# Output projection of a hybrid encoder block: row tiles normalised in the next step, gates three tiles ahead, operand sums stored by GpSimd

## The chip, the cores and the metric

The kernel runs on one core of a Trainium2 chip, in one launch. The metric is the device time of an execution in microseconds (us), median of several. The engines are named as the profile names them: PE (TensorE: matrix products and transposes), DVE (VectorE), ACT (ScalarE), POOL (GpSimd) and SP (SyncE, which here only issues loads). SBUF is the on-chip memory, PSUM the banks in which PE leaves its results.

## The reference

One layer of an encoder over 2048 rows of 1024 channels, all float32. Half of the mixing width (512 channels) comes from an mLSTM in two directions, half from a Hyena convolution. Each half is normalised in groups, both are concatenated and go through one output projection, whose result is normalised and added to x; then comes an MLP with 4096 inner channels. What matters here is the stretch between the two:

```python
def rms_norm(x, w):
    y = xf * rsqrt(mean(xf * xf, axis=-1) + EPS)
    return y * w
...
# ym: mLSTM output times its output gate, yz: convolution output times its gate
y  = concat(group_rms(ym, 4 heads), group_rms(yz, 8 groups))      # 2048 x 1024
x1 = x + rms_norm(y @ w_out, norm_mix_post)
h  = rms_norm(x1, norm_mlp_pre)
out = x1 + rms_norm(relu(h @ w_mlp_in)**2 @ w_mlp_out, norm_mlp_post)
```

## The kernel before

PE multiplies in three passes to keep float32 precision: each operand is split into a high and a low part (`hi`, `lo`), and `mm3` issues hi x hi, hi x lo and lo x hi (lines L159 to L161 of every group of rows). A split is a cast on ACT (L166) and a subtraction on DVE or POOL (L169).

`out_proj` works on 16 row tiles of 128 rows, in a loop of 18 steps (`for i in range(18)`). Five parts belong to a tile h:

- `gate(h)`: loads `rd` and `xg`, four matmuls into the bank `py` (L1247), DVE's product with `xg` gives `zt` (tile name `yz`), ACT's square (L1252), DVE's sum over groups (L1254), root and reciprocal (L239, L241), and POOL's scaling (L1257).
- `mixed(h)`: loads `ymt` and `ot`, POOL's product (L1329), then the same normalisation.
- `turned`: four transposes of such a tile into the bank `ptp` (L1263) and the split into `yt`, the operand of the projection.
- `part(po, e, y, k0)`: twelve matmuls of a half of the channels into accumulator bank `po[e]`. Three banks `po` and three banks `tp` (shared by `py`, `ptp` and `pto`) rotate.
- `finish(h, po)`: loads x into `xt`; ACT squares the accumulator (L1205), DVE scales it (L1211), POOL adds the residual (L1212): `xt` becomes x1 and is stored. `normed(h)`: ACT's square of x1 (L1351), DVE's scaling (L1354) into the tile `xo`. `turn_out(h)`: two tiles later in the loop, eight transposes into `pto`, and DVE's product (L1365) back into `xo`.

The MLP uses a fast form of a 2 x 2 block product with seven products, so `turn_out` of each odd tile also makes four sums and differences of blocks of an even and an odd tile (POOL, L1380 to L1383, in `tb` and `xo`) and stores five operands to `ht` in DRAM, each 256 KB as 512 rows of 512 bytes. The first step of the MLP (`first_step`, tiles `hm`, `cb`, `pm`, `m`) begins inside the loop's last two steps; its weights are prepared on POOL from tile 12 on (L1480 to L1490).

In the loop the order on PE, DVE and ACT is the order in which the code is written (`manual_schedule`). POOL's and SP's orders are set by a scheduler. Every engine takes its instructions in order. `self.load` issues from SP's queue, `self.store` from ACT's queue: there an issue is an instruction of ACT, and stands with its wait ahead of what follows on ACT. In the step of a tile, PE does: transposes of the next tile's `yz`, part 0 with `yz`, a gate's four matmuls, transposes of the next `ymt`, part 0 with `ym`, part 1 with `yz`, the eight transposes of `turn_out`, part 1 with `ym`.

Of the kernel before, what the change touches and what calls it, by code (L numbers as in the profile page):

```python
# [17 lines left out]
D = 1024  # L18
# [129 lines left out]
class Builder:  # L148
# [1127 lines left out]
    def out_proj(self, c):  # L1276
        tc, io = self.tc, self.io
        pe, dve, act, pool = self.pe, self.dve, self.act, self.pool
        wp = self.hq
        wl = c.enter_context(tc.tile_pool(name="owl", bufs=2))  # L1280
        gc = ExitStack()
        wk = gc.enter_context(tc.tile_pool(name="owk", bufs=2))
        ps = c.enter_context(tc.tile_pool(name="opt", bufs=3, space=PSUM, side="right"))
# [58 lines left out]
        def finish(h, po):  # L1342
            xt = wl.tile([128, D], F32, tag="xt", name="xt")
            self.load(xt, self.rows(io["x"][0], h))
            x1 = wl.tile([128, D], F32, tag="xo", name="xo", bufs=3)
            self.post(wl, po, wb, (x1[:, 0:512], x1[:, 512:1024]), xt, "po", dve if h == 15 else pool)
            self.store(self.x1[h], xt)
            return x1, xt

        def normed(h, x1, xt):  # L1350
            act.activation(x1, xt, AF.Square, accum_out=ss1[:, h:h + 1])  # L1351
            act.activation(ss1[:, h:h + 1], ss1[:, h:h + 1], AF.Sqrt, scale=1.0 / D, bias=self.eps)
            dve.reciprocal(r1[:, h:h + 1], ss1[:, h:h + 1])
            dve.tensor_scalar(x1, xt, r1[:, h:h + 1], None, ALU.mult)  # L1354
            return x1

        def turn_out(h, xn):

            xv = xn.rearrange("p (k c) -> p k c", k=8)
            for half in range(2):  # L1360
                ks = slice(4 * half, 4 * half + 4)
                pt = ps.tile([128, 512], F32, tag="tp", name="pto", bufs=3).rearrange("p (q c) -> p q c", q=4)
                for q in range(4):
                    pe.transpose(pt[:, q, :], xv[:, 4 * half + q, :], self.eye)
                dve.tensor_tensor(xv[:, ks, :], pt, self.nw1[:, ks].unsqueeze(2).to_broadcast([128, 4, 128]), ALU.mult)  # L1365
# [12 lines left out]
            b11, b21, b12, b22 = ev[:, 0:4, :], ev[:, 4:8, :], xv[:, 0:4, :], xv[:, 4:8, :]  # L1378
            ta, tb = (self.cb.tile([128, 2, 4, 128], F32, tag="cb", name="tb", bufs=9) for _ in range(2))
            pool.tensor_tensor(ta[:, 0], b12, b11, ALU.subtract)  # L1380
            pool.tensor_tensor(ta[:, 1], b22, ta[:, 0], ALU.subtract)
            pool.tensor_tensor(tb[:, 0], b21, ta[:, 1], ALU.subtract)
# [24 lines left out]
        self.load(wb, io["norm_mix_post"].partition_broadcast(128))  # L1407
        xns = {}
        staged = self.first_operands(scratch)
        for i in range(18):  # L1410
            with tc.manual_schedule(engines={mybir.EngineType.PE,mybir.EngineType.DVE,mybir.EngineType.Activation}):
                if i == 0:
                    ys[1] = mixed(1)
                    zs[2] = gate(2)
                    part(pos[0], 0, ym[0], 0)
                    ym[1] = turned(ys.pop(1), 1, 1)
                    ys[2] = mixed(2)
                elif i + 2 < 16:
# [3 lines left out]
                if i < 16:  # L1422
                    if i > 1:
                        pos[i] = banks()
                    if i > 1:
                        part(pos[i], 0, yz[i], 4)
# [480 lines left out]
```

## Time and profile before

| | |
|---|---|
| median of 3 runs | 2765.75 us (2764.37 to 2766.28) |
| profiled execution | 2761.93 us, span 2759.2 us, mean granted clock of PE 0.977 |
| PE busy | 2614.5 us, 95% of the span |
| DVE, ACT, POOL busy | 1523.9, 1220.6, 1189.9 us (55, 44, 43%) |
| 1225 to 1465 us (the loop): PE, POOL busy | 222.4 and 137.0 of 240 us |
| 1465 to 1525 us (first step of the MLP): PE busy | 46.1 of 60 us, at a clock of 0.83 |

The profile comes from one execution, a little under the median. In its rows a line such as `ptp<-eye,yz` reads "written from". A bracket `[4.52 <-POOL yz L1257]` behind a row is the time that the engine stood idle just before, and what ended it. Rows with a q (ACTq, SPq, POOLq) are instructions of that engine's queue, such as issues of DMAs. A profiled line of the changed kernel can stand one to two lines off its number before.

### The profile page before, as it was taken

Reading aid. Unit: us, or ns where it says so; the run is one execution under the profiler, and the core shown is the slowest. Engines: PE = TensorE matmul, PEld = TensorE weight load, DVE = VectorE, ACT = ScalarE, POOL = GpSimd, SP = SyncE. Lnnn points to the kernel's source line nnn. Section 1 sums busy time; section 2 is a strip of 40 time slices with the busy share of each in tenths; the row PEclk is TensorE's granted clock in tenths of the full one; section 3 lists DMA queues with packets and bytes.
Section 4 is the critical chain, followed back from the end, with each engine's and each line's share of the span. In section 5 each row is a group of like instructions: output and inputs, shape, how many; then the busy total and the mean of one; then the engine's idle time right before and its main releaser. Section 6 shows DMA issues by size and latency. Waiting matters only on the chain.

```text
span 2759.2 us, 35826 instructions
## 1 busy us (share of the span) xinstructions
PE 2614.5 (95%) x12422; PEld 2140.2 (78%) x12422; DVE 1523.9 (55%) x2598; ACT 1220.6 (44%) x2237; POOL 1189.9 (43%) x941
## 2 busy tenths in 40 slices
PE   6999999999899998789997999989999999999998
PEld 4778878777788888776775788868888888888876
DVE  5676643777546664664445445464445443543578
ACT  6355544555444444543334454454444233222244
POOL 1211114554225543424566777777773241311232
PEclk8999999999999999989998999999999999999999
DMA  6233336655566657956765544454446563445546
GB/s 169 62 91 108 115 115 211 196 186 178 195 218 179 183 164 243 269 177 195 229 189 190 180 141 163 151 207 167 144 151 229 198 184 108 121 143 158 188 154 227
DMA packets 307187, 474.22 MB, mean 172 GB/s; under 512 B 37814, under 2 KB 166198, under 8 KB 305984
## 3 DMA queue, kind: packets, MB, share of 16 engines
q1 hardware_dynamic: 231952, 333.24, 38.9%
q10 hardware_dynamic: 70304, 125.98, 12.1%
q0 software_dynamic: 4752, 12.72, 2.1%
q8 instruction: 99, 1.62, 0.2%
q14 instruction: 80, 0.66, 0.1%
HBM read 297.65 MB, written 174.20 MB: 171 GB/s over the span
## 4 chain that ended last, share of the span: by engine, by line
PE 44%; DMA 5%; DVE 4%; POOL 3%; issue 2%; ACT 1%; SPq 0%; ACTq 0%; DVEq 0%; POOLq 0%
PE pm L160 13%; PE pm L161 13%; PE pm L159 13%; DMA mb<-mrow 1%; DMA ymt<-ym 1%; POOL cb L169 1%; PE po L159 1%; PE po L160 1%; PE po L161 1%; PE py L1247 1%; DVE cb L169 1%; DMA m<-in_w_mlp_out_dram 1%; DVE hm L169 1%; DVE hm L1832 0%; PE pa L983 0%
## 5 line engine op out<-in xcount | busy, mean ns | idle before, releaser
L166 ACT CAST cb<-m 128x1024 fp32r<-128x1024 f32 (+1 forms) x346 | 281.3, 847 | 441.9 <-PE pm L159 388.1
L169 DVE TENSOR_TENSOR cb<-m,cb 128x1024 fp32r<-128x1024 f32 (+1 forms) x222 | 240.1, 1119 | 298.7 <-ACT cb L166 298.3
L159 PE MATMUL pm<-hm,cb 128*128 128x512 f32 x896 | 355.0, 396 | 16.9 <-ACT hm L166 5.8
L160 PE MATMUL pm<-hm,cb 128*128 128x512 f32 x896 | 355.1, 396 | 10.9 <-DVE hm L169 7.1
L161 PE MATMUL pm<-hm,cb 128*128 128x512 f32 x896 | 353.7, 395 | 0.0
L160 PE MATMUL pm<-cb 128*128 128x512 f32 x880 | 343.3, 390 | 7.2 <-DVE cb L169 7.2
L159 PE MATMUL pm<-cb 128*128 128x512 f32 x880 | 342.1, 389 | 1.0 <-DVE cb L169 1.0
L161 PE MATMUL pm<-cb 128*128 128x512 f32 x880 | 342.5, 389 | 0.0
L169 POOL TENSOR_TENSOR cb<-m,cb 128x1024 fp32r<-128x1024 f32 x124 | 273.7, 2221 | 73.3 <-ACT cb L166 62.5
L1644 DVE TENSOR_TENSOR m<-pm,m 128x512 f32<-128x512 f32 x224 | 154.3, 690 | 242.7 <-PE pm L161 218.5
L159 PE MATMUL pt<-hn,w 128*128 128x512 f32 x640 | 270.4, 423 | 1.0 <-ACT hn L487 0.9
L169 POOL TENSOR_TENSOR raw<-raw,hi 128x512 fp32r<-128x512 f32 x160 | 205.3, 1295 | 121.9 <-ACT hi L166 85.6
L160 PE MATMUL pt<-hn,w 128*128 128x512 f32 x640 | 254.7, 398 | 0.3 <-DVE hn L488 0.2
L161 PE MATMUL pt<-hn,w 128*128 128x512 f32 x640 | 253.2, 396 | 0.0
L159 PEld LDWEIGHTS pm<-hm,cb 128*128 128x128 f32 x896 | 171.1, 191 | 56.7 <-ACT hm L166 6.8
L160 PEld LDWEIGHTS pm<-hm,cb 128*128 128x128 f32 x896 | 170.9, 191 | 51.2 <-DVE hm L169 10.3
L160 PEld LDWEIGHTS pm<-cb 128*128 128x128 f32 x880 | 165.2, 188 | 44.7 <-DVE cb L169 10.6
L161 PEld LDWEIGHTS pm<-hm,cb 128*128 128x128 f32 x896 | 170.9, 191 | 36.4
L159 PEld LDWEIGHTS pm<-cb 128*128 128x128 f32 x880 | 165.1, 188 | 35.8 <-ACT junk L1817 1.4
L161 PEld LDWEIGHTS pm<-cb 128*128 128x128 f32 x880 | 165.2, 188 | 34.2
L1648 ACT ACTIVATE m<-m 128x512 f32<-128x512 f32 x128 | 80.5, 630 | 219.4 <-DVE m L1644 217.3
L597 DVE SCALAR_TENSOR_TENSOR yc<-pt,cw,yc 128x511 f32<-128x511 f32 (+1 forms) x280 | 135.1, 516 | 51.2 <-ACT yc L591 49.2
(321 smaller groups left out, 5604.2 us busy)
## 6 DMA issues: line engine op xcount, KB each, us to landing
ga<-m ACTq DMA_DIRECT2D x96, 512.0 KB, 4.4
m<-ga SPq DMA_DIRECT2D x96, 512.0 KB, 3.8
d<-st ACTq DMA_DIRECT2D x64, 512.0 KB, 4.0
m<-in_w_mlp_in_dram SPq DMA_DIRECT2D x62, 512.0 KB, 3.7
m<-in_w_mlp_out_dram SPq DMA_DIRECT2D x114, 256.0 KB, 4.0
raw<-d SPq DMA_DIRECT2D x96, 256.0 KB, 2.7
xt<-in_x_dram SPq DMA_DIRECT2D x32, 512.0 KB, 5.8
dk<-kst SPq DMA_DIRECT2D x32, 512.0 KB, 3.3
```

Of the source, the lines that this page charges most:

```text
L159: pe.matmul(ps, w[1], x[0], start=first, stop=False)
L160: pe.matmul(ps, w[0], x[1], start=False, stop=False)
L161: pe.matmul(ps, w[0], x[0], start=False, stop=last)
L166: self.act.copy(hi, src)
L169: (eng_lo or self.dve).tensor_tensor(lo, src, hi.bitcast(F32), ALU.subtract)
L597: dve.scalar_tensor_tensor(y[:, at], p[:, src], cw[:, ct, w:w + 1], y[:, at], ALU.mult, ALU.add)
L1247: self.pe.matmul(py, self.s1i[:, r], rd[:, r, :], start=r == 0, stop=r == 1)
L1644: dve.tensor_tensor(dst, a, b, ALU.add)
L1648: act.activation(g, g, AF.Relu)
```

## The change

- `normed(h)` moves out of the step of tile h, where it stood right behind `finish(h)`, into the next step, ahead of part 0 with `ym`. The store of x1 goes with it. `xo` has four places instead of three. The pool of `xt` and `xo` is opened just ahead of the loop, on the other side of SBUF.
- `gate` runs three tiles ahead instead of two (`yz` has three places; step 0 does two gates). `mixed(i + 2)` stands behind part 0 with `ym` instead of at the head of a step.
- Of the five operands of an odd tile, one (3) stays a store of ACT's queue; the four sums are issued by `pool.dma_start`, on POOL's own queue. The first goes out behind its sum, the other three behind the last sum.

PE has the same instructions in the same number.

```diff
@@ out_proj
-        wl = c.enter_context(tc.tile_pool(name="owl", bufs=2))
...
-            zt = wk.tile([128, 512], F32, tag="yz", name="yz")
+            zt = wk.tile([128, 512], F32, tag="yz", name="yz", bufs=3)
...
-            x1 = wl.tile([128, D], F32, tag="xo", name="xo", bufs=3)
+            x1 = wl.tile([128, D], F32, tag="xo", name="xo", bufs=4)
             self.post(wl, po, wb, (x1[:, 0:512], x1[:, 512:1024]), xt, "po", dve if h == 15 else pool)
+            return x1, xt
+
+        def normed(h, x1, xt):
             self.store(self.x1[h], xt)
-            return x1, xt
-
-        def normed(h, x1, xt):
             act.activation(x1, xt, AF.Square, accum_out=ss1[:, h:h + 1])
...
-            for i, src in ((3, b22), (5, ta[:, 0]), (7, b12), (6, ta[:, 1]), (4, tb[:, 0])):
-                out(i, src)
+            out(3, b22)
+            for i, src in ((5, ta[:, 0]), (6, ta[:, 1]), (4, tb[:, 0]), (7, b12)):
+                pool.dma_start(self.ht[h // 8, i - 1][:, :, 128 * t:128 * t + 128], src)
...
+        wl = c.enter_context(tc.tile_pool(name="owl", bufs=2, side="right"))
         for i in range(18):
...
                     ym[1] = turned(ys.pop(1), 1, 1)
+                    zs[3] = gate(3)
                     ys[2] = mixed(2)
-                elif i + 2 < 16:
-                    ys[i + 2] = mixed(i + 2)
                 if 0 < i < 15:
                     yz[i + 1] = turned(zs.pop(i + 1), i + 1, 0)
...
-                if 0 < i < 14:
-                    zs[i + 2] = gate(i + 2)
+                if 1 < i < 16:
+                    pos[i] = banks()
+                    part(pos[i], 0, yz[i], 4)
                 if 0 < i < 15:
+                    if i + 3 < 16:
+                        zs[i + 3] = gate(i + 3)
                     ym[i + 1] = turned(ys.pop(i + 1), i + 1, 1)
                 if 0 < i < 16:
+                    xns[i - 1] = normed(i - 1, *done)
                     part(pos[i], 0, ym[i], 0)
+                    if i + 2 < 16:
+                        ys[i + 2] = mixed(i + 2)
                     if i > 1:
                         part(pos[i], 1, yz[i], 4)
                 if 2 <= i:
                     turn_out(i - 2, xns.pop(i - 2))
                 if i < 15:
                     part(pos[i], 1, ym[i], 0)
-                    xns[i] = normed(i, *finish(i, pos.pop(i)))
+                    done = finish(i, pos.pop(i))
```

On ACT, in the step that turns tile 5 out, before: the five stores of operands (`xo_12969` is tile 5), then the accumulator of tile 7 (`xo_13244`), the store of its x1 and its square.

```order
L234 DMA ht_84<-xo_12969 512x1x128
L234 DMA ht_84<-tb_13219 512x1x128
L234 DMA ht_84<-xo_12969 512x1x128
L234 DMA ht_84<-tb_13219 512x1x128
L234 DMA ht_84<-tb_13220 512x1x128
L1205 ACTIVATE xo_13244,pss_13245<-po0_13145 128x512
L1205 ACTIVATE xo_13244,pss_13245<-po1_13146 128x512
L166 CAST yt_13279<-ptp_13280 128x512
L239 ACTIVATE po_sd_13250<-ps1_13248,eps_60 128x1
L234 DMA x1_83<-xt_13242 128x1024
L1351 ACTIVATE xo_13244,ss1_12126<-xt_13242 128x1024
```

The same place after (`xo_12986` is tile 5, `xo_13261` and `xt_13259` tile 7; `xg`, `gr64` belong to a gate):

```order
L234 DMA ht_84<-xo_12986 512x1x128
L1205 ACTIVATE xo_13261,pss_13262<-po0_13144 128x512
L1205 ACTIVATE xo_13261,pss_13262<-po1_13145 128x512
L166 CAST yt_13278<-ptp_13279 128x512
L239 ACTIVATE po_sd_13267<-ps1_13265,eps_60 128x1
L1252 ACTIVATE xg_13301<-yz_13304 128x512
L239 ACTIVATE gr64_sd_13312<-gss_13310,eps_60 128x8
L166 CAST yt_13278<-ptp_13317 128x512
L234 DMA x1_83<-xt_13259 128x1024
L1350 ACTIVATE xo_13261,ss1_12123<-xt_13259 128x1024
```

Four stores are gone ahead of L1205, and the store and the square of x1 stand behind the gate's square and the cast of the second `ptp`.

On POOL, around the sums of tile 5, before (`yz_13163` is tile 9, `ymt_13266` tile 10, `xt_13242` tile 7):

```order
L1257 TENSOR_TENSOR yz_13163<-yz_13163,gr64_r_13173 128x512
L1380 TENSOR_TENSOR tb_13219<-xo_12969,xo_12827 128x512
L1381 TENSOR_TENSOR tb_13219<-xo_12969,tb_13219 128x512
L1383 TENSOR_TENSOR xo_12969<-xo_12969 128x512
L1382 TENSOR_TENSOR tb_13220<-xo_12827,tb_13219 128x512
L1257 TENSOR_TENSOR ymt_13266<-ymt_13266,gr128_r_13276 128x512
L1212 TENSOR_TENSOR xt_13242<-xo_13244,xt_13242 128x512 x2
```

After (`ymt_13199` is tile 9, `ymt_13341` tile 10, `xt_13259` tile 7):

```order
L1257 TENSOR_TENSOR ymt_13199<-ymt_13199,gr128_r_13209 128x512
L1379 TENSOR_TENSOR tb_13236<-xo_12986,xo_12844 128x512
L1385 DMA ht_84<-tb_13236 512x1x128
L1380 TENSOR_TENSOR tb_13236<-xo_12986,tb_13236 128x512
L1382 TENSOR_TENSOR xo_12986<-xo_12986 128x512
L1381 TENSOR_TENSOR tb_13237<-xo_12844,tb_13236 128x512
L1385 DMA ht_84<-tb_13236 512x1x128
L1385 DMA ht_84<-tb_13237 512x1x128
L1385 DMA ht_84<-xo_12986 512x1x128
L1212 TENSOR_TENSOR xt_13259<-xo_13261,xt_13259 128x512
L1328 TENSOR_TENSOR ymt_13341<-ymt_13341,ot_13342 128x512
L1212 TENSOR_TENSOR xt_13259<-xo_13261,xt_13259 128x512
```

Four issues stand between the sums and the residual sum of the tile that was multiplied in that step, and the product of tile 10's `ymt` has come to stand behind them.

On SP, at the loop's beginning, before (`ot_12300` and `ymt_12299` are tile 2, the `xg` and `rd` are of gates):

```order
L231 DMA rd_12476<-d21_3602 128x2x512
L231 DMA xg_12264<-vp2_76 128x1x512
L231 DMA ot_12300<-vo_79 128x1x512
L231 DMA ymt_12299<-ym_82 128x1x512
L231 DMA rd_12609<-d21_3602 128x2x512
```

After (`ot_12317` and `ymt_12316` are tile 2, `xg_12264` and `xg_12300` of the gates of tiles 2 and 3):

```order
L231 DMA xg_12264<-vp2_76 128x1x512
L231 DMA xg_12300<-vp2_76 128x1x512
L231 DMA ymt_12316<-ym_82 128x1x512
L231 DMA rd_12475<-d21_3602 128x2x512
L231 DMA ot_12317<-vo_79 128x1x512
```

A second gate's `xg` now stands ahead of tile 2's `ot`, which rotates through the same two places.

More of the change, by code (lines that the diff above doesn't have):

```diff
@@ L1344, in finish @@
             self.load(xt, self.rows(io["x"][0], h))
-            x1 = wl.tile([128, D], F32, tag="xo", name="xo", bufs=3)
+            x1 = wl.tile([128, D], F32, tag="xo", name="xo", bufs=4)
             self.post(wl, po, wb, (x1[:, 0:512], x1[:, 512:1024]), xt, "po", dve if h == 15 else pool)
-            self.store(self.x1[h], xt)
             return x1, xt
         def normed(h, x1, xt):
+            self.store(self.x1[h], xt)
             act.activation(x1, xt, AF.Square, accum_out=ss1[:, h:h + 1])
@@ L1416, in out_proj @@
                     ym[1] = turned(ys.pop(1), 1, 1)
+                    zs[3] = gate(3)
                     ys[2] = mixed(2)
-                elif i + 2 < 16:
-                    ys[i + 2] = mixed(i + 2)
                 if 0 < i < 15:
                     yz[i + 1] = turned(zs.pop(i + 1), i + 1, 0)
[L1422 to L1426, printed above, removed]
-                if 0 < i < 14:
-                    zs[i + 2] = gate(i + 2)
+                if 1 < i < 16:
+                    pos[i] = banks()
+                    part(pos[i], 0, yz[i], 4)
                 if 0 < i < 15:
+                    if i + 3 < 16:
+                        zs[i + 3] = gate(i + 3)
                     ym[i + 1] = turned(ys.pop(i + 1), i + 1, 1)
                 if 0 < i < 16:
+                    xns[i - 1] = normed(i - 1, *done)
                     part(pos[i], 0, ym[i], 0)
+                    if i + 2 < 16:
+                        ys[i + 2] = mixed(i + 2)
                     if i > 1:
```

## The prediction

> **What bounds the kernel now.** I began with a table of the stage in stretches of 60 us, since the page's shares average over stages with different limits. The loop over row tiles runs from about 1225 us to 1470 us, the MLP's first step follows. Columns: PE, PEld, DVE, ACT and POOL busy (instructions), then the granted clock, the DMA share and GB/s.
>
> ```profile
> 1405.00:1465.00 60.00, 56.19 (x262) 43.84 (x261) 24.81 (x51) 22.22 (x53) 40.36 (x31) 1.00 0.53 165
> 1465.00:1525.00 60.00, 46.09 (x175) 35.24 (x174) 30.85 (x36) 22.58 (x34) 30.42 (x19) 0.83 0.66 223
> ```
>
> PE is the bound, and it is not full: it lacks 4 us of the loop's last 60 and 14 us of the 60 that follow. No other engine is near its limit; POOL is nearest, with 40 of 60 us just ahead of the MLP. What the change can win is therefore the sum of PE's gaps. The timeline of PE shows each with its releaser in brackets:
>
> ```profile
> 1251.95 1.11 PE L1263 MATMUL ptp<-eye,yz 128*128 128x128 f32 x4 [4.52 <-POOL yz L1257]
> 1291.73 0.50 PE L159 MATMUL po<-wo,yt 128*128 128x512 f32 x1 [0.71 <-DVE xo L1211]
> 1299.75 0.66 PE L1263 MATMUL ptp<-eye,yz 128*128 128x128 f32 x4 [1.32 <-DVE xo L1365]
> 1330.75 0.66 PE L1263 MATMUL ptp<-eye,yz 128*128 128x128 f32 x4 [1.27 <-DVE xo L1365]
> 1361.35 0.66 PE L1263 MATMUL ptp<-eye,yz 128*128 128x128 f32 x4 [1.14 <-DVE xo L1365]
> 1380.81 0.66 PE L1263 MATMUL ptp<-eye,yz 128*128 128x128 f32 x4 [4.62 <-POOL yz L1257]
> 1421.22 0.50 PE L159 MATMUL po<-wo,yt 128*128 128x512 f32 x1 [0.63 <-DVE xo L1211]
> 1429.25 0.66 PE L1263 MATMUL ptp<-eye,yz 128*128 128x128 f32 x4 [1.32 <-DVE xo L1365]
> 1451.90 0.50 PE L159 MATMUL po<-wo,yt 128*128 128x512 f32 x1 [1.36 <-DVE xo L1211]
> 1464.70 0.51 PE L159 MATMUL po<-wo,yt 128*128 128x512 f32 x1 [0.50 <-DVE xo L1211]
> ```
>
> They add up to 17.4 us. The two long ones cost more than their length, since the clock drops behind them (same columns as the first table):
>
> ```profile
> 1251.95:1256.00 4.05, 4.05 (x14) 3.39 (x15) 2.22 (x5) 0.88 (x2) 3.56 (x3) 0.61 0.53 184
> 1380.80:1385.00 4.20, 4.19 (x14) 3.38 (x15) 0.00 (x0) 0.00 (x0) 4.12 (x4) 0.59 0.57 196
> ```
>
> At 0.61 and 0.59 of full speed that is 4.05 x 0.39 + 4.20 x 0.41 = 3.3 us. So the loop loses 20.7 us in all. Why the short gaps arise stands in the waits (engine, line, what was awaited: total, times, longest) and on ACT's timeline:
>
> ```profile
> ACT xo L1351 <- POOL xt L1212: 56.3, 14, 5.8
> ...
> 1385.15 1.37 ACTq L234 DMA_DIRECT2D ht<-tb  x2
> 1386.63 0.60 ACT L1205 ACTIVATE xo<-po 128x512 f32<-128x512 f32 x1 [7.62 <-POOL tb L1382]
> ...
> 1467.74 1.06 ACT L1351 ACTIVATE xo<-xt 128x1024 f32<-128x1024 f32 x1 [4.07 <-POOL xt L1212]
> ```
>
> ACT takes its work in order. On every odd tile the stores of sums stand in its queue ahead of the next squares (L1205), and each must wait until POOL has made its sum; here ACT did no arithmetic for 7.62 us. Every tile has a second stop: the square of L1351 stands right behind its own tile's residual sum on POOL, 56.3 us of waiting in 14 tiles (not all of it harmful: the next squares may not be due yet). Both delay L1205, then DVE's L1211, which frees the accumulator's bank, and DVE's L1365, which frees a bank of the ring of three for transposes.
>
> **The change, part by part.** *The stores of sums leave ACT's queue* (4 of 5 on each of 8 odd tiles). This takes the first stop away: the remaining store needs only DVE's L1365. *Normalising one step later* takes the second away: the residual sum has most of a step to be made before ACT arrives at the square. With both gone I count the six gaps of the loop behind L1365 or L1211 up to 1430 us as gone: 0.71 + 1.32 + 1.27 + 1.14 + 0.63 + 1.32, or 6.4 us. Four places for normalised rows only pay for a tile's longer life, in space. The store of x1 and the last reader of xt move a step back too, so the load of x two tiles on goes out later: it still has over a step (14.6 us, below), and the waits show nothing of it.
>
> *Gate three tiles ahead.* Both long gaps are waits for yz, the gate's rows, on POOL. The second begins with a late load:
>
> ```profile
> 1375.17 1.28 POOL L1329 TENSOR_TENSOR ymt<-ymt,ot 128x512 f32<-128x512 f32 x1 [6.54 <-DMA ymt<-ym]
> ```
>
> POOL stood 6.54 us at the load of another tile, with yz queued behind it. One tile more of lead is 14.6 us (below), more than that, so yz is no longer what ends last: 4.52 + 4.62 + 3.3 us of clock = 12.4 us go. But the normed operand ymt is now the next one late. At the start its buffer comes from the ring xg that the gates use too, and the change gives it a later place there:
>
> ```profile
> 1234.71 0.69 DVE L1254 TENSOR_REDUCE gss<-xg 128x8 f32<-128x512 f32 x1 [0.75 <-ACT xg L1252]
> ...
> 1234.95 1.29 POOL L1329 TENSOR_TENSOR ymt<-ymt,ot 128x512 f32<-128x512 f32 x1 [3.03 <-DMA ymt<-ym]
> ...
> 1239.10 1.04 POOL L1257 TENSOR_TENSOR ymt<-ymt,gr_r 128x512 f32<-128x512 f32 x1 [1.85 <-DVE gr_r L241]
> ...
> 1239.54 1.88 PE L1247 MATMUL py<-rd,s1i 128*128 128x512 f32 x4
> 1241.26 0.60 PE L1263 MATMUL ptp<-eye,ymt 128*128 128x128 f32 x4
> ...
> ot<-vo SPq DMA_DIRECT2D x14, 256.0 KB, 4.8
> ```
>
> The last line is of the DMA view: the median load of ot lands 4.8 us after its issue. The buffer is free when the reduction of xg is done, at 1235.4, so the load lands at 1240.2. From the product to the end of the scaling an earlier ymt took 1234.95 to 1240.14, 5.2 us, with another scaling of POOL in between; I take 4.4 and get 1244.6. PE was at the transpose of ymt at 1241.26 and has one gate more to do before it (1239.54 to 1241.26, 1.7 us), so it arrives at about 1242.9: a new gap of 1.8 us. Its bounds are 0 and the 4.52 that it replaces. For the clock behind it I add 0.7, half of what followed the long gaps. The page "TensorE: Matmul & The Clock Gate" of the Trainium skill, Part 1, says that the clock falls only after an idle window of about 3.4 us; by that the 0.7 would be nothing and the time 0.7 us lower, which the two rows above, both behind longer gaps, can't decide.
>
> At the 4.62 gap the load of ymt remains late, now without yz behind it, and POOL has the MLP's two splits to do (2.45 us in a row below): between 0 and 4.6 us, and I take 1, since ymt is wanted later in a step than yz. In other steps, mixed stands later in its step: its loads come behind the gate's on SP's queue, its product behind the residual sum on POOL. Landing and chain (4.8 + 5.2 us) fit into the step of 14.6 us that it still has: nothing.
>
> *DMAs issued by POOL.* Before has none in this stage; POOL's own work there is (mean ns behind the bar):
>
> ```profile
> L1212 POOL TENSOR_TENSOR xt<-xo,xt 128x512 f32<-128x512 f32 x29 | 36.9, 1290 | 33.6 <-DVE xo L1211 33.6
> L1329 POOL TENSOR_TENSOR ymt<-ymt,ot 128x512 f32<-128x512 f32 x16 | 20.5, 1284 | 22.7 <-DMA ymt<-ym 20.4 <-issue 2.2
> L1257 POOL TENSOR_TENSOR ymt<-ymt,gr_r 128x512 f32<-128x512 f32 x16 | 16.6, 1040 | 13.8 <-DVE gr_r L241 13.7
> L1257 POOL TENSOR_TENSOR yz<-yz,gr_r 128x512 f32<-128x512 f32 x14 | 16.1, 1146 | 27.2 <-DVE gr_r L241 23.3 <-DMA ymt<-ym 3.9
> L1380 POOL TENSOR_TENSOR tb<-xo 128x512 f32<-128x512 f32 x6 | 7.7, 1288 | 4.5 <-DVE xo L1365 4.5
> ...
> L631 POOL DMA_DIRECT2D vp<-vst x96 | 61.2, 642 | 220.5 <-ACT vst L627 219.4 <-issue 1.1
> ...
> L185 POOL DMA_DIRECT2D cs1k<-in_c_s1k_dram x1 | 0.7, 731 | 0.1
> ```
>
> The nearest rows are the 96 of an early stage: 128 KB as 256 rows of 512 bytes in 0.64 us. Those of the change have 256 KB, 512 such rows. Between no growth and growth with the rows an issue costs 0.64 to 1.27 us. The constant's DMA, 128 KB as 128 rows, took 0.73, so fewer rows were not cheaper, and I take a value near the lower end, 0.8. Four make 3.2 us of POOL on each odd tile. Whether it is covered follows from the step's length, which two transposes of a quiet odd step give, and from where its sums begin:
>
> ```profile
> 1268.07 0.60 PE L1263 MATMUL ptp<-eye,yz 128*128 128x128 f32 x4
> ...
> 1282.68 0.60 PE L1263 MATMUL ptp<-eye,yz 128*128 128x128 f32 x4
> ...
> 1282.39 1.29 POOL L1380 TENSOR_TENSOR tb<-xo 128x512 f32<-128x512 f32 x1 [2.06 <-DVE xo L1365]
> ```
>
> A step is 14.6 us. In two steps POOL has 2 x (2 x 1.29 + 1.28 + 1.04 + 1.15) + 4 x 1.29 = 17.3 of 29.2 us, which leaves 11.9 us, 3.0 for each of the four. In order it is tighter. Counted from the step's first transpose, the sums begin at 14.3 and end at 19.5; then come four issues of x, two residual sums (2.6) and ACT's square (1.1): 23.2 + 4x. The next square of the accumulator, behind it on ACT, is wanted at 29.2, when the next step's last product is done. So an issue is hidden up to x = 1.5 us, above both bounds: nothing in quiet steps.
>
> In the last three steps, where POOL also prepares the MLP's weights (the 40.36 us of the first table), that cover is thin. I leave the two gaps of 1.36 and 0.50 there and add one issue, 0.64: 2.5 us. Bounds: 0, and 5 if all four issues come to lie on the path.
>
> *The MLP's first step.* Its casts stand behind the stores of tile 13's sums on ACT, too:
>
> ```profile
> 1480.01 0.58 ACT L1657 COPY m<-pm 128x512 f32<-128x512 f32 x1 [10.79 <-DMA ht<-tb]
> ...
> 1491.17 0.80 PE L159 MATMUL pm<-hm,cb 128*128 128x512 f32 x1 [2.66 <-ACT hm L166]
> 1492.43 0.80 PE L160 MATMUL pm<-hm,cb 128*128 128x512 f32 x1 [0.46 <-DVE hm L169]
> ...
> 1482.57 2.45 POOL L169 TENSOR_TENSOR hm<-hm,hm 128x1024 fp32r<-128x1024 f32 x1 [3.40 <-ACT hm L166]
> ```
>
> With the stores gone ACT casts earlier, and 2.66 + 0.46 = 3.1 us go. Against it, POOL's split of the same operands comes behind four issues more; it waited 3.4 us for ACT there (last row), about what the issues take. Range -4 to +10 us, the latter if the slow clock of this stretch (0.83) goes as well.
>
> **The sum.** Loop 20.7 - (1.8 + 0.7 + 1.0 + 2.5) = 14.7, first step 3.1: 17.8 us. The profiled execution took 2761.93 us, so 2744.1; the median of the runs is 2765.75, 3.8 above it, so 2748. About 0.2% (5.5 us) is what a measurement can tell from no change.
>
> **The rivals.** *POOL late before the MLP* (two issues' queues and weights together): the term of 2.5 us becomes 5 and the first step loses 4 instead of gaining 3.1, 9.6 us less: 2757. For it speaks POOL's 40 of 60 us, against it its wait of 3.4 us.
>
> *Slower: POOL's issues are held up.* From x = 1.5 us each odd tile costs 4 (x - 1.5) us on PE, on seven tiles of the loop. At x = 2.35 this eats 17.8 us and another 6, and the kernel is slower; at 2.5, for example, it takes 28 us and gives 2776. The mechanism would be DVE shutting POOL out while it normalises from memory to memory:
>
> ```profile
> L1354 DVE TENSOR_SCALAR xo<-xt,r 128x1024 f32<-128x1024 f32 x14 | 13.0, 926 | 0.9
> ```
>
> One such instruction per tile, 0.93 us, can hold one issue of the four, not all, and none of the 96 early issues can have been held long at a mean of 0.64 us. The Trainium skill, "SBUF — State Buffer", under "SBUF: two separate sides", warns of just this: GpSimd can't write descriptors while VectorE runs an instruction that takes both ports, and the section "A bandwidth-pool intuition that's wrong" puts a DMA of 620 ns at 3100 ns beside a copy. With 3.1 us for x the formula gives 45 us and 2793, as an estimate by that page.
>
> *No change: the gaps only move.* yz comes early, but ymt is then what is late, by as much (12.4 us with the clock), the first step gains nothing, and the last three steps lose their bound of 5. 20.7 - 17.4 = 3.3 us remain: 2762. For it speaks that the load of ymt at 1375 us is late whatever the gate does.
>
> *More.* The first step's slow clock goes with its waits (+7): 2741 or less.
>
> **How the numbers follow.** Forecast 0.62; POOL late 0.14; gaps only move 0.11; POOL held up 0.06; more 0.07. Faster by over 0.2% are the forecast, the extra gain and nearly all of the first rival: 0.81. Same are most of the third and a little of the first: 0.13. Slower: 0.06. The range runs from 2738 (half of the 6 us that the loop gives back stays won, and the 7 of the first step's clock) to 2762 (gaps only move); the likeliest case by itself has 2741 to 2755.
>
> **What would show it.** In the profile after: no wait of L1205 for a sum's store; the square of L1350 waiting little for L1212; no gap of PE for yz; a gap of about 2 us for ymt near 1243; POOL's issues at 0.6 to 1.3 us; gaps behind L1211 in the last three steps. I am wrong if issues take over 1.5 us, or if ymt takes the place of yz in PE's waits.

## The result, and the profile after

The changed kernel takes 2751.81 us (median of 4 runs, 2747.24 to 2753.09), against 2765.06 us (4 runs) of the kernel before beside it. The ratio is 0.9948, with a 95% interval of 0.9936 to 0.9960: 0.52% faster. The forecast was 2748, with a range of 2738 to 2762. The profiled execution took 2752.2 us with a span of 2750.3 us, so the two profiles differ by 9.7 us, less than the medians (13.3): that of before was at the fast end of its runs.

First the same table of stretches (PE, PEld, DVE, ACT, POOL busy, clock, DMA share, GB/s), after:

```profile
1405.00:1465.00 60.00, 53.65 (x247) 42.58 (x246) 29.89 (x45) 19.07 (x43) 48.57 (x39) 0.97 0.56 180
1465.00:1525.00 60.00, 45.31 (x173) 34.26 (x172) 37.14 (x38) 25.31 (x37) 35.89 (x27) 0.86 0.55 189
```

PE was not made fuller there. POOL went from 40.4 to 48.6 of 60 us ahead of the MLP. The gain lies earlier. All gaps of PE in the loop, from PE's timeline of the changed kernel:

```profile
1243.89 0.66 PE L1263 MATMUL ptp<-eye,ymt 128*128 128x128 f32 x4 [0.89 <-POOL ymt L1257]
1372.53 2.73 PE L1247 MATMUL py<-rd,s1i 128*128 128x512 f32 x4 [1.85 <-DVE xo L1364]
1389.45 1.98 PE L1247 MATMUL py<-rd,s1i 128*128 128x512 f32 x4 [0.38 <-DVE xo L1364]
1410.07 0.50 PE L159 MATMUL po<-wo,yt 128*128 128x512 f32 x1 [0.80 <-DVE xo L1211]
1422.09 0.66 PE L1263 MATMUL ptp<-eye,ymt 128*128 128x128 f32 x4 [2.07 <-POOL ymt L1257]
1439.54 0.50 PE L159 MATMUL po<-wo,yt 128*128 128x512 f32 x1 [1.10 <-DVE xo L1211]
1454.22 0.50 PE L159 MATMUL po<-wo,yt 128*128 128x512 f32 x1 [2.38 <-DVE xo L1211]
```

They make 9.5 us, against 17.4. Between 1245 and 1370 us PE has no gap at all; everything that is left comes in the step with the first MLP splits and in the last steps. The clock behind some of them (same columns as the first table):

```profile
1240.00:1246.00 6.00, 5.11 (x23) 3.34 (x22) 3.75 (x10) 4.02 (x12) 3.09 (x4) 1.00 0.74 228
1372.00:1378.00 6.00, 5.47 (x15) 3.50 (x16) 4.08 (x8) 1.91 (x7) 5.71 (x6) 0.72 0.74 219
1456.00:1462.00 6.00, 6.00 (x26) 4.86 (x25) 2.11 (x4) 1.45 (x3) 2.73 (x3) 0.75 0.99 332
```

Two of them cost 0.28 x 6.0 = 1.7 and 0.25 x 6.0 = 1.5 us more. So the loop loses 12.7 us now, 8.0 less than the 20.7 of before. The MLP's first matmul and a later one of its first step, before and after, show how much was won up to each:

```profile
1471.25 0.39 PE L159 MATMUL pm<-hm,cb 128*128 128x512 f32 x1
1544.00 0.50 PE L159 MATMUL pm<-hm,cb 128*128 128x512 f32 x1 [1.56 <-POOL cb L169]
```

```profile
1462.34 0.39 PE L159 MATMUL pm<-hm,cb 128*128 128x512 f32 x1
1533.57 0.50 PE L159 MATMUL pm<-hm,cb 128*128 128x512 f32 x1 [1.57 <-POOL cb L169]
```

8.9 us are won by the first, 10.4 us by the second: the first step itself gave 1.5 us. Counted from the loop's first matmul (1223.57 and 1223.69) it is 9.0 and 10.5 us, with the same work of PE in between. The spans differ by 8.9 us, so 1.5 us are lost again behind the second mark, where the change alters nothing. Between the two marks PE stood idle for 17.5 us before and 17.5 after; what the first step gave is the clock, 0.86 there before (72.75 us) and 0.88 after (71.23 us). The waits of the changed kernel (total, times, longest) and POOL's issues (count, busy, mean ns):

```profile
DVE r L1352 <- ACT ss L1351: 37.4, 13, 6.3
ACT xo L1350 <- POOL xt L1212: 32.0, 10, 5.2
ACT po_sd L239 <- DVE ps L1207: 17.5, 8, 3.7
...
L1385 POOL DMA_DIRECT2D ht<-tb x24 | 18.0, 797 | 3.2 <-POOL tb L1379 1.8 <-issue 1.5
...
L1385 POOL DMA_DIRECT2D ht<-xo x8 | 7.9, 987 | 0.0
```

The wait of L1205 for a sum is gone, and that of the square for the residual sum fell from 56.3 to 32.0 us. Two waits have come up: DVE's for the root of the normalising (L1352, 7.9 us before, with `turn_out`'s product queued behind it), and ACT's for DVE's addition L1207 of two numbers per row.

### The profile page after: what moved, and what is told of

It is laid out like the page before. It is cut to its first block, busy times and chain, and to the rows that moved or that the text cites. A ratio compares the mean times of both kernels' runs of the same rounds, so it can differ in the third digit from the quotient of the medians.

```text
span 2750.3 us, 35835 instructions
## 1 busy us (share of the span) xinstructions
PE 2608.7 (95%) x12422; PEld 2137.5 (78%) x12422; DVE 1536.1 (56%) x2598; ACT 1224.0 (45%) x2237; POOL 1213.8 (44%) x973
## 3 DMA queue, kind: packets, MB, share of 16 engines
q8 instruction: 99, 1.62, 0.2%
## 4 chain that ended last, share of the span: by engine, by line
PE 39%; DVE 5%; POOL 4%; ACT 2%; DMA 2%; issue 2%; ACTq 0%; DVEq 0%; SPq 0%; POOLq 0%
PE pm L160 13%; PE pm L161 13%; PE pm L159 13%; DVE cb L169 1%; POOL xt L1212 1%; DVE hm L169 1%; POOL cb L169 1%; ACT xo L1350 1%; DVE hm L1834 1%; DMA m<-in_w_mlp_out_dram 0%; DMA m<-in_w_mlp_in_dram 0%; DMA hm<-ht 0%; DVE xo L1353 0%; ACTq L234 0%; POOL ht L1385 0%
```

## The experiments

Ratios are to the kernel before on the same chip, with 95% intervals. The last column is read from one profiled execution of each kernel: the time from the loop's first matmul to the second mark above (320.4 us before), with the same number of matmuls in between. What lies ahead of the loop and behind the mark differed by up to 7.6 and 5.0 us between these profiles, though the edits leave it as it is, so a median can show more or less than the loop does. POOL's order came out of the scheduler anew for every kernel, and in some of them it differs from that of the changed kernel. The parts do not add up:

| kernel | ratio | median us | to the mark, us |
|---|---|---|---|
| changed kernel | 0.9948 (0.9936 to 0.9960) | 2751.81 | 309.9 |
| before + gate three ahead | 0.9966 (0.9956 to 0.9977) | 2760.09 | 315.4 |
| before + POOL's stores | 1.0036 (1.0021 to 1.0051) | 2777.93 | 338.3 |
| before + POOL's stores + four places | 1.0064 (1.0050 to 1.0079) | 2784.50 | 345.9 |
| before + normalising later + four places | 0.9990 (0.9979 to 1.0001) | 2764.25 | 323.3 |
| changed, stores on ACT as before | 0.9966 (0.9954 to 0.9979) | 2758.07 | 316.3 |
| changed, stores on ACT a step later | 1.0003 (0.9994 to 1.0013) | 2766.87 | 324.7 |
| changed, three places | 1.0006 (0.9995 to 1.0017) | 2767.47 | 327.6 |
| changed, gate two ahead | 0.9946 (0.9928 to 0.9965) | 2751.40 | 313.4 |
| changed, POOL's issues doubled | 1.0042 (1.0027 to 1.0056) | 2777.99 | 332.6 |
| changed + L1207 as a reduction | 0.9941 (0.9929 to 0.9953) | 2752.04 | 310.7 |
| the same + splits on DVE | 0.9944 (0.9932 to 0.9957) | 2750.36 | 307.6 |
| the same + two residual sums on DVE | 0.9932 (0.9919 to 0.9944) | 2747.55 | 306.7 |

**The gate's lead alone.**

```diff
-            zt = wk.tile([128, 512], F32, tag="yz", name="yz")
+            zt = wk.tile([128, 512], F32, tag="yz", name="yz", bufs=3)
...
+                    zs[3] = gate(3)
                     ys[2] = mixed(2)
...
-                if 0 < i < 14:
-                    zs[i + 2] = gate(i + 2)
+                if 0 < i < 13:
+                    zs[i + 3] = gate(i + 3)
```

> The kernel before, with nothing but the gate three tiles ahead (three places for yz). Theory A: the gaps behind yz (4.5, 4.6 us and 3.3 us of clock) go, and about 2 us each come back as waits for ymt: 2756 to 2760; the short gaps of 1.1 to 1.4 us stay. Rival (ymt is as late as yz was): 2764 to 2766, with gaps of 4 us at the transpose of ymt.

Measured 2760.09, ratio 0.9966. PE's timeline has no gap for yz on POOL in the loop; the two that matter are:

```profile
1247.69 0.66 PE L1263 MATMUL ptp<-eye,ymt 128*128 128x128 f32 x4 [0.58 <-POOL ymt L1257]
...
1389.02 0.80 PE L159 MATMUL po<-wo,yt 128*128 128x512 f32 x1 [6.03 <-DVE xo L1211]
```

At the start ymt takes the place of yz for 0.58 us, less than expected. In the split step the gap only moves: 6.03 us at the accumulator's bank in place of 4.62 at yz. The ratio stands for 9 us, of which the profile shows 5.0 up to the mark; where the others lie is open.

**The gate's lead taken out of the change.**

```diff
-            zt = wk.tile([128, 512], F32, tag="yz", name="yz", bufs=3)
+            zt = wk.tile([128, 512], F32, tag="yz", name="yz")
...
-                    zs[3] = gate(3)
...
-                    if i + 3 < 16:
-                        zs[i + 3] = gate(i + 3)
+                    if i + 2 < 16:
+                        zs[i + 2] = gate(i + 2)
```

> The changed kernel with the gate two tiles ahead, as before, and two places for yz; normalising in the next step, four places for xo and POOL's stores stay. Alone on the kernel before, the gate's lead gave 0.34%. Theory A (it breaks the wait of PE for yz behind a late POOL, which POOL's stores make later still): gaps behind yz come back on several odd steps, 2763 to 2775. Rival (the parts add up): 2752 plus 9, 2761, with just the two gaps behind yz at the start and in the split step.

Both fail: 2751.40, 0.9946, the time of the changed kernel. The waits for yz come back, but small, and another gap grows:

```profile
1384.93 0.66 PE L1263 MATMUL ptp<-eye,yz 128*128 128x128 f32 x4 [2.90 <-POOL yz L1257]
...
1455.28 0.79 PE L159 MATMUL po<-wo,yt 128*128 128x512 f32 x1 [6.77 <-DVE xo L1211]
```

There is no long gap for yz at the start. So in this company the gate's lead is worth nothing that the medians can show, which here is anything under about 5 us; by the mark of the two profiles it is worth 3.5 us. What keeps the start free of the gap without it is not separated: this kernel keeps `mixed` later in its step, which no run tried alone.

**POOL's stores alone.**

```diff
-            for i, src in ((3, b22), (5, ta[:, 0]), (7, b12), (6, ta[:, 1]), (4, tb[:, 0])):
-                out(i, src)
+            out(3, b22)
+            for i, src in ((5, ta[:, 0]), (6, ta[:, 1]), (4, tb[:, 0]), (7, b12)):
+                pool.dma_start(self.ht[h // 8, i - 1][:, :, 128 * t:128 * t + 128], src)
```

> The kernel before, with nothing but the four stores of sums moved to POOL's queue. Theory A: the short gaps of the loop behind L1365 and L1211 (6.4 us) go, but not the two gaps behind yz (12.4 us with their clock): 2759 to 2761, and L1207 becomes long (about 4 us) on odd tiles where it meets the sums. Rival: with the square still in its own step ACT waits there instead, and the short gaps stay: 2764 to 2766.

Slower by 0.36%, which neither expected. A wait and a gap of this kernel:

```profile
ACT xo L1205 <- POOL tb L1382: 37.6, 6, 7.6
...
1468.95 0.80 PE L159 MATMUL po<-wo,yt 128*128 128x512 f32 x1 [4.43 <-DVE xo L1211]
```

The stores no longer stand ahead of L1205, and it still waits for L1382, six times and up to 7.6 us. L1205 writes its squares into the tile xo, and with three places that is the place of the even tile which L1382 reads. The queue was one of two holds; the ring was the other.

**With a fourth place.** The edit above, the pool of `xt` and `xo` opened just ahead of the loop on the other side, so that it fits, and:

```diff
-            x1 = wl.tile([128, D], F32, tag="xo", name="xo", bufs=3)
+            x1 = wl.tile([128, D], F32, tag="xo", name="xo", bufs=4)
```

> The kernel before with the stores of sums on POOL's queue and four places for xo; normalising in its own step, gate two ahead. Three places with these stores took 1.0036 of the time of before, and there L1205 waited 37.6 us in all for L1382, a reader of the place that it writes. Theory R (ring): with four places that wait goes, and the kernel is 5 to 10 us faster than with three, at or under before (2760 to 2768). Theory Q (four issues a tile make POOL late for everything): still 8 to 12 us over before.

Slower still, 1.0064, by more than either theory said. The wait for L1382 did go, and this stands in its place:

```profile
ACT xo L1350 <- POOL xt L1212: 73.0, 13, 10.6
...
1369.47 1.12 PE L1263 MATMUL ptp<-eye,yz 128*128 128x128 f32 x4 [5.77 <-POOL yz L1257]
```

Normalising in its own step, ACT takes up its square early and then stands still for the residual sum, which comes on POOL behind sums and issues: 73.0 us of waiting, against 56.3 before. The gate's square is queued behind it, so yz comes late.

**Normalising later alone** (with four places).

```diff
-            self.store(self.x1[h], xt)
             return x1, xt
...
         def normed(h, x1, xt):
+            self.store(self.x1[h], xt)
...
+                    xns[i - 1] = normed(i - 1, *done)
                     part(pos[i], 0, ym[i], 0)
...
-                    xns[i] = normed(i, *finish(i, pos.pop(i)))
+                    done = finish(i, pos.pop(i))
```

> The kernel before with the normalising one step later and four places for xo, no other part of the change (the pool of xt and xo opens just ahead of the loop, on the other side, so that it fits). The hold of ACT behind the sums has two candidate causes: the stores of sums in ACT's queue, and the ring of three places, in which the square's target (L1205) is the place of the even tile that POOL still reads. Theory Q (queue): ACT still waits 6 to 8 us on odd tiles for the stores, the two gaps behind yz stay, and the time is that of before within 0.1%. Theory R (ring): the fourth place frees L1205 and 3 to 6 us go.

2764.25, ratio 0.9990, as theory Q had it. The second hold shrank from 56.3 us of waiting to 18.3, the first stays:

```profile
ACT xo L1350 <- POOL xt L1212: 18.3, 7, 6.2
...
ACT xo L1205 <- POOL tb L1381: 14.9, 2, 7.6
```

**The stores back on ACT.** The edit of turn_out undone in the changed kernel.

> The changed kernel, with the four stores of sums back on ACT's queue in the order of before. Theory A (the stores held ACT, and PE through it): ACT's L1205 waits 6 to 8 us on odd tiles again, gaps of 1.1 to 1.3 us of PE return on five or more odd steps and the first step loses some more: 2757 to 2762. Rival: the gate's lead alone made the gain, and with the square one step later nobody waits for ACT: 2752, as the changed kernel.

2758.07, 0.9966: POOL's stores are worth about 0.18% in the company of the rest. The intervals overlap a little (0.9954 to 0.9960); the mark gives 6.4 us, as the medians do. The time is theory A's, its short gaps are not: there are none from 1260 to 1370 us. The loss is in a few large ones:

```profile
1384.16 0.80 PE L159 MATMUL po<-wo,yt 128*128 128x512 f32 x1 [5.76 <-DVE xo L1211]
...
1481.58 0.77 PE L159 MATMUL pm<-hm,cb 128*128 128x512 f32 x1 [8.04 <-issue]
```

**Three places in the changed kernel.**

```diff
-            x1 = wl.tile([128, D], F32, tag="xo", name="xo", bufs=4)
+            x1 = wl.tile([128, D], F32, tag="xo", name="xo", bufs=3)
```

> The changed kernel with three places for xo instead of four. Theory R: L1205 waits for POOL's sums and issues again, by 4 us or more on each odd tile, and most of the gain goes: 2760 to 2775. Theory Q (the fourth place only pays for the longer life of a tile and costs nothing but space): L1205 waits no longer than in the changed kernel, 2752 to 2754.

2767.47, the whole gain gone. Theory R holds here:

```profile
ACT xo L1205 <- POOL tb L1381: 29.0, 7, 7.9
...
1455.79 0.80 PE L159 MATMUL po<-wo,yt 128*128 128x512 f32 x1 [6.97 <-DVE xo L1211]
```

**The stores on ACT, a step later.**

```diff
             out(3, b22)
-            for i, src in ((5, ta[:, 0]), (6, ta[:, 1]), (4, tb[:, 0]), (7, b12)):
-                pool.dma_start(self.ht[h // 8, i - 1][:, :, 128 * t:128 * t + 128], src)
+            late.append((out, ((5, ta[:, 0]), (6, ta[:, 1]), (4, tb[:, 0]), (7, b12))))
...
                     xns[i - 1] = normed(i - 1, *done)
+                    flush()
...
```

`flush()` issues what `late` has collected; it is also called in the last two steps.

> The changed kernel with the four stores of sums back on ACT's queue, but written one step later, behind the normalising of the next tile, when the sums are long made. POOL loses its four issues per odd tile (3.4 us), ACT gets four issues of 0.5 to 0.6 us. Theory A (POOL's lateness in the split step and the last steps makes the gaps that are left): gaps behind L1211 and L1364 after 1370 us shrink from 6.5 to 3 us, L1207 no longer meets issues between the sums, and the time is 2 to 5 us under the changed kernel. Rival (ACT's issues are in the way of L1205 by as much): the same time within 1 us.

2766.87, 15 us over the changed kernel: both fail. ACT's and PE's timelines:

```profile
1445.58 1.06 ACT L1350 ACTIVATE xo<-xt 128x1024 f32<-128x1024 f32 x1 [7.39 <-POOL xt L1212]
...
1449.39 1.35 ACTq L234 DMA_DIRECT2D ht<-tb  x2
...
1453.99 0.60 ACT L1205 ACTIVATE xo<-po 128x512 f32<-128x512 f32 x1 [4.35 <-DMA ht<-tb]
...
1456.82 0.80 PE L159 MATMUL po<-wo,yt 128*128 128x512 f32 x1 [6.58 <-DVE xo L1211]
...
1534.91 0.79 PE L159 MATMUL pm<-hm,cb 128*128 128x512 f32 x1 [4.81 <-POOL cb L169]
```

The late stores take 0.5 to 0.7 us each to issue (1.35 for two), ahead of L1205. ACT's square waits 7.39 us there for the residual sum on POOL (5.2 at most in the changed kernel), although POOL no longer issues anything for the sums: its lateness is not that of the issues alone. Of the 14.8 us lost up to the mark, 5.2 lie in the loop and 7.2 behind 1510 us. There `tb`, which shares its ring with the MLP's operands `cb`, is held longer, and ACT has four late stores among the MLP's casts. Which of the two delays the weights was not separated.

**POOL's issues doubled.**

```diff
-                pool.dma_start(self.ht[h // 8, i - 1][:, :, 128 * t:128 * t + 128], src)
+                for to in (self.ht, self.ht2):
+                    pool.dma_start(to[h // 8, i - 1][:, :, 128 * t:128 * t + 128], src)
```

> The changed kernel in which POOL issues each of the four sums twice, the second time to a DRAM tensor that nobody reads: 3.4 us more of POOL on each odd tile (0.85 us an issue, measured), as if x were 1.7. Theory A (the prediction's: an issue is hidden up to 1.5 us in quiet steps): about 4 x 0.2 = 0.8 us on each of the first five odd tiles, and several us in the last steps and the first of the MLP, where POOL has no room: 2757 to 2766. Rival (POOL is in time everywhere and the remaining gaps come from elsewhere): 2752 to 2754. Third (each issue is on the path already): 8 odd tiles by 3.4 us, 2779.

2777.99, beside the third theory's 2779, but not for its reason, as the rows show. First POOL's product, sums and issues, the normalising and PE's stall in this kernel, then the same place of the changed kernel:

```profile
1306.05 1.29 POOL L1329 TENSOR_TENSOR ymt<-ymt,ot 128x512 f32<-128x512 f32 x1 [5.77 <-DMA ot<-vo]
...
1322.23 3.75 POOL L1387 DMA_DIRECT2D ht<-tb  x5
1325.42 2.04 POOL L1387 DMA_DIRECT2D ht<-xo  x2
...
1331.93 0.16 DVE L1353 RECIPROCAL r<-ss 128x1 f32<-128x1 f32 x1 [8.67 <-ACT ss L1352]
...
1334.79 3.78 PE L1248 MATMUL py<-rd,s1i 128*128 128x512 f32 x4 [4.75 <-DVE xo L1365]
```

```profile
1298.44 1.28 POOL L1328 TENSOR_TENSOR ymt<-ymt,ot 128x512 f32<-128x512 f32 x1 [3.06 <-DMA ot<-vo]
...
1321.59 0.16 DVE L1352 RECIPROCAL r<-ss 128x1 f32<-128x1 f32 x1 [2.25 <-ACT ss L1351]
...
1323.65 1.25 DVE L1364 TENSOR_TENSOR xo<-pto,nw 128x512 f32<-128x512 f32 x2
...
1326.63 1.88 PE L1247 MATMUL py<-rd,s1i 128*128 128x512 f32 x4
```

Five issues take 1322.23 to 1325.42: 0.64 us each (the spans of a row overlap). So doubling adds 2.6 us a tile. In the changed kernel the first half of DVE's product L1364 is done at about 1324.3, and PE needs its bank at 1326.63: 2.3 us of slack. POOL's lateness passes through ACT's square to DVE, which stands 8.67 us at the root with the product queued behind, and PE stalls 4.75 us for a bank.

The loop of this kernel runs 3.2 us later at this place, by the transposes of the step (1326.64 and 1323.39). So the root came 7.1 us later than in the changed kernel, not 2.6: POOL had begun the sums of this tile 4.2 us late already. It had waited 5.77 us for a load of `ot`, whose place the product of the step before had freed later. That product came later behind the doubled issues and also because the scheduler moved it behind both residual sums and a scaling. What the order adds, and what the 8 MB of second writes add, is not separated from the issues. The first odd tile cost PE nothing; after that come three stalls of 4.6 to 6.0 us, at 1334.79, 1403.92 and 1441.61, and one of 5.0 at 1477.85. By the granted clock of the five stretches of 60 us from 1225 to 1525 us, the slow clock cost about 23 us here and 13 in the changed kernel, so some 10 of the 26 us are clock.

**L1207 as a reduction over one operand.**

```diff
-        self.dve.tensor_tensor(s1, ss[:, 0:1], ss[:, 1:2], ALU.add)
+        if tag == "po":
+            self.dve.tensor_reduce(s1, ss, AX.X, ALU.add)
+        else:
+            self.dve.tensor_tensor(s1, ss[:, 0:1], ss[:, 1:2], ALU.add)
```

> The changed kernel, with the add of the two square sums (L1207, two small operands in SBUF) written as a reduction over one operand; nothing else differs. Theory A (DVE can't start an instruction with two SBUF operands while POOL runs its sums): L1207 took 3.7 to 4.1 us on four odd tiles; as a reduction it takes under 0.3 us everywhere, the gaps of PE behind L1211 (0.80, 1.10, part of 2.38) go, and the time falls by 2 to 4 us against the changed kernel (2751.8). Theory B (POOL is simply late with its own work): L1207 waits for a result and not for a port, it stays long or another instruction takes its place, and the time is unchanged within 1 us.

In the changed kernel (first fence, with POOL's sums and issues) and in this one (with a sum of POOL):

```profile
1404.44 4.12 DVE L1207 TENSOR_TENSOR ps<-pss 128x1 f32<-128x1 f32 x1 [1.98 <-ACT xo L1205]
...
1404.73 1.32 POOL L1380 TENSOR_TENSOR tb<-xo,tb 128x512 f32<-128x512 f32 x1
...
1408.43 1.53 POOL L1385 DMA_DIRECT2D ht<-tb  x2
```

```profile
1283.16 1.33 POOL L1383 TENSOR_TENSOR tb<-xo,tb 128x512 f32<-128x512 f32 x1
1283.35 0.15 DVE L1208 TENSOR_REDUCE ps<-pss 128x1 f32<-128x2 f32 x1 [2.50 <-ACT xo L1205]
...
1456.97 0.51 PE L159 MATMUL po<-wo,yt 128*128 128x512 f32 x1 [3.65 <-DVE xo L1214]
```

The mechanism of theory A is shown: an addition of one element per row took 4.12 us, until POOL turned from its sums to its issues (3.71 at the tile of the second fence), and takes 0.15 us in the middle of such a sum when it reads one operand. The gaps of 0.80 and 1.10 us went. The time did not move: the gap near 1455 grew from 2.38 to 3.65, that at 1389 from 0.38 to 2.05. The wait was real and was not what ended last.

**Splits of operands 6 and 5 on DVE,** with the reduction.

```diff
-        self.right_split(6, self.pool)
+        self.right_split(6)
...
-        self.right_split(5, self.pool)
+        self.right_split(5)
```

> The changed kernel with L1207 as a reduction and, in the MLP's first step, the second halves of the splits of operands 6 and 5 on DVE instead of POOL. Theory A (there DVE's L1212 took 4.93 us beside POOL's two splits, locked out): no DVE instruction takes over 2.5 us there, the first step's gaps (14.3 us with the last of them) shrink by 3 to 6 us: 2746 to 2749. Rival (the loads of the operands, at a DMA share of 1.02, end last): the gaps stay and the time is 2751 to 2753.

DVE's residual sum of tile 15 in the changed kernel, beside POOL's splits, and in this one:

```profile
1472.41 4.93 DVE L1212 TENSOR_TENSOR xt<-xo,xt 128x512 f32<-128x512 f32 x1
```

```profile
1471.61 1.54 DVE L1215 TENSOR_TENSOR xt<-xo,xt 128x512 f32<-128x512 f32 x1
```

The lock is gone there but for one sum of POOL, yet the first step's gaps only went from 14.3 to 12.8 us, and 2750.36 (0.9944) is not to be told from the kernel without it. The mark shows 3.1 us, which the medians (1.7 us) do not make sure.

**Residual sums of tiles 13 and 14 on DVE** in addition.

```diff
-            self.post(wl, po, wb, (x1[:, 0:512], x1[:, 512:1024]), xt, "po", dve if h == 15 else pool)
+            self.post(wl, po, wb, (x1[:, 0:512], x1[:, 512:1024]), xt, "po", dve if h >= 13 else pool)
```

> The kernel with the reduction and the splits on DVE, and in addition the residual sums of tiles 13 and 14 on DVE, as tile 15's is. In the changed kernel ACT waited 4.75 and 3.98 us for these sums on POOL, which has the splits of the MLP's weights between them, and PE then 2.38 us. Theory A (POOL's order in the last steps): the gap of 2.4 to 3.7 us near 1455 us goes with its slow clock, 2 to 5 us under the same kernel without it. Rival (DVE, with two operands in SBUF, is locked out by POOL's splits for as long): no change within 1 us, and these sums take 3 us and more on DVE.

2747.55, ratio 0.9932: the lowest of all, 2.8 us under the kernel without it on the same chip, though its interval still meets that of the changed kernel. The time is that of theory A, the mechanism is not:

```profile
1440.72 6.24 DVE L1215 TENSOR_TENSOR xt<-xo,xt 128x512 f32<-128x512 f32 x1
...
1455.87 0.50 PE L159 MATMUL po<-wo,yt 128*128 128x512 f32 x1 [1.62 <-DVE xo L1214]
```

One sum took 6.24 us beside POOL's splits, as the rival said, and the gap near 1455 did not shrink (1.35 without, 1.62 with it). At the mark of the first step used above (1530.69 and 1530.33) only 0.9 us of the 2.8 is won, counted from the loop's first matmul (1223.13 and 1223.63). Where the rest lies is not settled.

## Why the prediction was right, and where its steps failed

The sign, the size (13 of 18 us) and the range were right. That the time came so near is in part luck: up to the mark the two profiles show 10.5 of the 17.8 us; the medians differ by 13.3 because the profiled execution of before lies 3.8 us under its median. By steps, against the profile:

- *The short gaps* (6.4 us): right; none is left up to 1370 us. But the square of L1350 still waited 32.0 us for L1212, not little, as forecast; up to there that cost PE nothing.
- *Both long gaps go, by the gate's lead* (12.4 us): they went, but the lead does not decide it. Alone it takes away the first and only moves the second (0.34% in all). Taken out of the change, the first stays away and gaps of 2.90 and 1.55 us for yz come back in the second's place, which costs nothing by the medians and 3.5 us by the mark.
- *Four places only pay for a longer life, in space*: wrong. With three, all of the gain is lost. I looked at ACT's queue and not at the place that the square writes into; L1205's rows name a sum of POOL as releaser, which fits both.
- *An issue of POOL at 0.8 us*: the rows show 0.80 and 0.99, and the distance between issues is 0.64 us. That is the lower bound: no growth from 256 to 512 rows of 512 bytes.
- *Hidden up to 1.5 us*: too much. I followed POOL's lateness to ACT's L1205 and left out DVE, where the root of the normalising now stands ahead of `turn_out`'s product. There the slack was 2.3 us in a quiet step, which hides an issue up to 0.64 + 2.3/4 = 1.2 us if POOL starts on time. I also left out that a late POOL makes the next step late, through the load of `ot`; with the issues doubled that was the larger part.
- *The start* (1.8 + 0.7 us): 0.89, at full clock. (The working itself gives 1.7, and half of the 1.6 us behind a long gap is 0.8; the sum of 2.5 stays.) The page "TensorE: Matmul & The Clock Gate" of the Trainium skill, Part 1, fits this one, where no drop followed a gap of 0.89 us. But 1.85 us at 1372 were followed by a clock of 0.72, which the rule as I put it, an idle window of some 3.4 us, does not give. What the traces show in its place stands in the last section.
- *The split step* (1.0 us): 1.85 + 0.38 and 1.7 of clock, 3.9. *The last steps* (2.5 us): 0.80 + 2.07 + 1.10 + 2.38 and 1.5 of clock, 7.9. These are the two terms that were sized too low, 8.3 us together, beyond the bound of 5 for the last steps. POOL's two late splits were priced by POOL's time, not by DVE's product queued behind normalising. The 0.80 and 1.10 are DVE's wait in L1207, a term that the sum did not have.
- *The first step* (3.1 us): 1.5, and not by the waits that were to go: its gaps were 13.9 us before and are 14.3 now, and the 1.5 us are clock. ACT casts earlier, but DVE's split and residual sum met POOL's sums and splits and took 4.17 and 4.93 us.

The sum by these rows: 20.7 - 12.7 = 8.0 in the loop and 1.5 behind it, 9.5 us, against 10.5 up to the mark. The other 1.0 us is PE's busy time in the loop (230.04 and 229.03 us), which the rows do not explain. That 9.5 lies so near to the 9.7 us between the profiled executions is chance, since 1.5 us are lost again behind the mark.

Of the rivals, *POOL late before the MLP* happened in the loop beyond its own bound (7.9 us against 5) and not in the first step. *POOL's issues held up by DVE* was not put to the test: in the nine kernels that store from POOL, none of the issues overlaps in time with DVE's normalising from memory to memory. So the warning of the page "SBUF — State Buffer" in the Trainium skill, under "SBUF: two separate sides", is neither borne out nor refuted by these runs. What they show is a hold the other way round: POOL's sums held DVE.

## What to carry to other kernels

When a wait is moved off a queue, look for its second cause: the ring place that the waiting instruction writes, and the engine on which the late result is taken up next. Parts of such a change can be a loss alone (1.0036, 1.0064) and a gain together (0.9948), because each only opens one of several holds in a row; test them by taking one out of the whole, not only by putting one in. And slack has to be followed through every in-order engine down to PE, since the shortest one counts, and on into the next step, where a load that was issued late passes the lateness on.

## What the runs showed of the hardware

- An instruction of DVE with two operands in SBUF waited as long as POOL went on with its sums, three in a row: 4.12 us for 128 x 1 elements, 0.15 us when it reads one operand. Sums of 128 x 512 took 4.93 and 6.24 us, beside two splits of POOL in a row, instead of 0.68. The Trainium skill has the shared port as a lock held for one whole instruction ("SBUF — State Buffer", "SBUF: two separate sides"); here the wait went over several.
- Within a row of issues POOL issued 256 KB in 512 rows in 0.64 us, the time that 128 KB in 256 rows took.
- An issue on ACT took 0.52 us alone and about 0.65 us when others stood just ahead of it (1.35 us for two); with the DMA engines at a share of 0.96 four took 1.2 to 1.6 us each.
- In all fourteen traces the clock was granted either in full or at 0.50, the latter for 3.41 us or a multiple of it, and within a trace the slow stretches lie on one grid of 3.41 us (1373.63 and 1455.55 in the changed kernel, 24 such steps apart). From 1230 to 1560 us, every stretch of this grid at full clock in which PE stood idle for over 1.85 us was followed by a slow one, and none with under 1.79 was. So the idle time within one stretch counted, not the length of a gap: 1.85 us inside one stretch of the changed kernel cost 1.7 us of clock, while 2.07 there and 2.90 in the kernel with the gate two ahead lay across the border of two and cost none.
